# Products of row-tile pairs with seven multiplications instead of eight: which pairs take them, and where the weight sums are kept

## The chip, the core and the metric

The kernel runs on one core of a Trainium2 chip. The core has a matrix engine (TensorE, PE in the profile, with PEld for its weight loads), VectorE (DVE), ScalarE (ACT), GpSimd (POOL) and a queue engine (SyncE, SP) that issues the transfers from device memory into the on-chip buffer. Matrix products add up in a separate memory of accumulators (PSUM). The metric is the device time of one execution in microseconds. Before the change it was 2223.25 us, the median of 3 runs (2222.24 to 2224.91).

## The reference

The program is a trunk of two pre-norm layers on 256 tokens of width 2048, in float32. Each layer has a token mixer (layer 0: neighbourhood attention, layer 1: a gated short convolution) and a gated MLP with a convolution over the tokens between its two projections. A last norm closes it.

```python
def conv_glu_ffn(x, w_up, conv_w, conv_b, w_down):
    h = dwconv_centered(x @ w_up, conv_w) + conv_b      # w_up 2048 x 11264
    g, u = jnp.split(h, 2, axis=-1)
    return (jax.nn.silu(g) * u) @ w_down                # w_down 5632 x 2048

def short_conv_mixer(x, w_in, conv_w, w_out):
    gb, gc, h = jnp.split(x @ w_in, 3, axis=-1)
    return (gb * dwconv_centered(gc * h, conv_w)) @ w_out

for i in range(2):
    a = rms_norm(h, mix_norm[i])
    h = h + (neighborhood_attention(a, ...) if i == 0 else short_conv_mixer(a, ...))
    h = h + conv_glu_ffn(rms_norm(h, ffn_norm[i]), ...)
return rms_norm(h, final_norm)
```

## The kernel before

Every float32 number is held as a high and a low part, and a product of two numbers is made of three matmuls: high by high, high by low and low by high. The high part of a weight is made by ScalarE (`hi`, L122) and the low part by VectorE (`lo`, L123), out of a loaded chunk of 512 KB in one of five buffers named `raw`; `hi` and `lo` have six buffers each. `prep_to` issues the load and the splits of a chunk some steps ahead of its use (`AHEAD = 4` chunks).

Two kinds of stages follow one another. A `Phase` holds weights still and streams all tokens past them (the up-projections, L160 and L164); VectorE and ScalarE finish its columns (L213 to L225). A `Tokens` stage holds the tokens still and streams weights past them, 512 columns at a time (L336 to L338): the attention's output, the short convolution's output (`in_wscout`) and, twice in each MLP, one half of the down-projection (`in_wdown`, 22 of the 44 row tiles of the weight each). These four halves are called here L0h0, L0h1, L1h0 and L1h1, by layer and half.

A `Tokens` stage walks over two column groups (g = 0 and 1, 1024 columns each). In a group it takes its row tiles of weights two by two: 11 pairs in half an MLP, counted here from index 0, so that index 1 is the second pair. Four accumulators (`mm`: two token blocks by two halves of the columns) collect the products. A pair takes 8 products, of three matmuls each, on two chunks ("left" and "right", by columns). In a pair whose index is in a set (`S_DOWN`, L41; `S_OUT`), the 2 by 2 blocks are multiplied with seven products instead (`seven`): the two chunks are added to one another in four ways on VectorE (`sums`, L132 to L135), the tokens' sums (`forms`) were made in the stage before, and the seven products go partly into the four `mm` accumulators and partly into four more (`mu`, under the tags `st`, `sc`, `tr`, `o`). One pair after the last seven of a group, `combine` (L362 to L370) adds the four `mu` accumulators to the residual `h`. When a group's last pair is done, `residual` (L244) adds each `mm` accumulator to `h`, which frees it for the next group.

In stages that end in a norm (L0h1, `in_wscout`, the attention's output), the first group's half of the norm's input is transposed on PE into accumulators under the same four tags (L255) and scaled by VectorE and ScalarE (`scaled_split`, L200 and L201) while the second group runs. The first seven of that group needs these four accumulators back. The last half, L1h1, ends with `finale`: its last two pairs are done accumulator by accumulator, so that the final norm (`last_evac`: transposes L606, the statistic L618 to L622, its broadcast `bc` L624, eight multiplies per token block L631 and the output's transfers) can begin before the last product.

A scheduler sets each engine's order of instructions from priorities and its own estimates, so the order is not that of the code. Engines work strictly in their order.

Of the kernel before, what the change touches and what calls it, by code (L numbers as in the profile page):

```python
# [15 lines left out]
F32 = mybir.dt.float32  # L16
# [6 lines left out]
P = 128  # L23
D = 2048
S = 256
KT = D // P
# [4 lines left out]
HALF = FT // 2  # L31
# [3 lines left out]
CH = 8  # L35
# [4 lines left out]

S_DOWN = (2, 4, 6, 8)  # L41
S_OUT = (1, 3, 5)


# [10 lines left out]
def trunk(ctx, tc, xT, par, bias, wqk, wv, wo, wsc, wscout, wup, wdown, out):  # L55
    nc = tc.nc
    cp = ctx.enter_context(tc.tile_pool(name="const", bufs=1))
    wp = ctx.enter_context(tc.tile_pool(name="wts", bufs=1))
    ap_ = ctx.enter_context(tc.tile_pool(name="acts", bufs=1))
    tp = ctx.enter_context(tc.tile_pool(name="tmp", bufs=2))  # L60
# [35 lines left out]
    prepped = []  # L96
# [29 lines left out]
    def sums(l, r):  # L126

        t13 = wp.tile([P, CH * P], F32, name="raw", tag="raw", bufs=5)
        t24 = tp.tile([P, CH * P], F32, name="t24", tag="qk")
        v13, v24 = (x.rearrange("p (k f c) -> p f k c", f=4, c=P) for x in (t13, t24))  # L130
        add = nc.vector.tensor_add
        add(out=v13[:, :, 0, :], in0=l[:, :, 0, :], in1=r[:, :, 0, :])  # L132
        add(out=v13[:, :, 1, :], in0=r[:, :, 1, :], in1=r[:, :, 0, :])
        add(out=v24[:, :, 0, :], in0=v13[:, :, 0, :], in1=r[:, :, 1, :])  # L134
        add(out=v24[:, :, 1, :], in0=v24[:, :, 0, :], in1=l[:, :, 1, :])  # L135
        return parts(r[:, :, 1:2, :]), parts(t13), parts(t24)

# [132 lines left out]
    class Tokens:  # L270

        def __init__(self, parts, src, evac, sset=(), forms=None, halves=0):


            self.src, self.evac, self.sset, self.forms = src, evac, sset, forms
            self.halves = halves
            self.nk = sum(n for _, n in parts)
            for g in range(KT // 8):  # L280
                base = 0
                for w, n in parts:
                    for k0 in range(0, n, 2):
# [9 lines left out]
                        chunks.append((left, 8 * P, "cols"))  # L293
                        if k // 2 in sset:
                            chunks.append((right, 8 * P, "sums"))
                            items.append((self, g, c + 1, k, k, k + 2))
                            ends.append(c + 2)
                        else:
                            chunks.append((right, 8 * P, "cols"))
                            items.append((self, g, c, k, k, k + 2))  # L300
                            items.append((self, g, c + 1, k, k, k + 2))
                            ends.extend((c + 1, c + 2))
                    base += n

        def run(self, g, c, k0, ka, kb):
            if kb - ka > 2:
                return self.finale(g, c, ka)
            if k0 // 2 in self.sset:
                return self.seven(g, c, k0)
# [30 lines left out]
        def seven(self, g, c, k0):  # L340
            i = k0 // 2
            first, last = i == min(self.sset), i == max(self.sset)
            if first:
                self.u = [pa.tile([P, 4 * P], F32, name="mu", tag=n) for n in ("st", "sc", "tr", "o")]
            a, e, f, b = self.u
            left, (w22, t13, t24) = prepped[c - 1], prepped[c]
            fh, fl = (self.forms[i][:, j * 4 * P:(j + 1) * 4 * P] for j in range(2))
            s1, s2, s4, s3 = ((fh[:, j * P:(j + 1) * P], fl[:, j * P:(j + 1) * P]) for j in range(4))
            raw = lambda k, t: tuple(self.src[k0 + k][:, j + t * P:j + (t + 1) * P] for j in (0, S))
            for ps, x, w, j in ((a, raw(0, 0), left, 0), (self.c["11"], raw(1, 0), left, 1), (self.c["12"], s4, w22, 0),  # L350
                                (e, s1, t13, 0), (f, s3, t13, 1), (b, s2, t24, 0), (self.c["21"], raw(1, 1), t24, 1)):
                own = ps in self.u
                self.product(ps, *x, *(y[:, j * 4 * P:(j + 1) * 4 * P] for y in w[:2]), own and first, own and last)
# [298 lines left out]
    def mlp(layer, a, evac):  # L652
        for half in range(2):
# [3 lines left out]
                  intro=0 if half else 3)  # L657
            Tokens([(wdown[layer, half], HALF)], act, evac if half else residual, S_DOWN, forms,
                   halves=4 if half and layer else 0)
# [6 lines left out]
    Phase(wsc, range(3 * KT), KT, a2, sc_evac, intro=3)  # L666
    Tokens([(wscout, KT)], yT, to_norm(3, a3), S_OUT, yforms)
    mlp(1, a3, last_evac())


# [112 lines left out]
```

## Time and profile before

| what | value |
|---|---|
| median of 3 runs | 2223.25 us |
| the profiled execution, its time and its span | 2225.79 us, 2224.0 us |
| granted TensorE clock, share of full speed | 0.998 |
| PE busy | 2204.5 us, 99% |
| VectorE busy | 1748.4 us, 79% |
| ScalarE busy | 1264.9 us, 57% |
| GpSimd busy | 92.3 us, 4% |
| loads of `in_wdown` | 176 of 512 KB, median 4.8 us to landing |
| sums of weight chunks, L132 | 38, and as many of L133, L134 and L135 |

Busy time is the time in which an engine works on an instruction; the span is the time from the first instruction to the last. A row of the timeline gives the start and the duration of an instruction; in square brackets stands how long the engine had been idle before it, and what released it.

### The profile page before, as it was taken

How to read it: one execution, taken by the hardware profiler on the slowest of the kernel's cores; microseconds unless marked ns; L12 is line 12 of the kernel's file. 1: busy time of each engine (PE TensorE's matmuls, PEld its weight loads, DVE VectorE, ACT ScalarE, POOL GpSimd, SP SyncE). 2: the span in 40 equal slices, each digit the busy share in tenths (PEclk: the TensorE clock that was granted, in tenths of full speed). 3: DMA queues.
4: the chain of work that ended last, by engine and by line, in shares of the span. 5: the costliest groups of instructions: out<-in, count | busy, mean ns of one | idle time of the engine just before them, and what ended most of it. 6: DMA issues, size and time to landing. Idle time of an engine off the chain costs nothing.

```text
span 2224.0 us, 31804 instructions
## 1 busy us (share of the span) xinstructions
PE 2204.5 (99%) x11794; PEld 1902.7 (86%) x11794; DVE 1748.4 (79%) x2619; ACT 1264.9 (57%) x1881; POOL 92.3 (4%) x103
## 2 busy tenths in 40 slices
PE   9999999999999999999999999999999999999997
PEld 8888888888888888888788888888888878888886
DVE  8777665788788877888886767888787888787887
ACT  7555544656555565665564444566566555665554
POOL 1011000000100001000000000000100000001000
PEclk9999999999999999999999999999999999999999
DMA  8656555555556755665665555565566566565564
GB/s 270 191 181 184 177 172 189 181 187 192 189 169 195 232 188 180 194 190 175 182 218 191 188 189 174 180 216 189 181 194 185 175 201 218 186 192 184 170 185 137
DMA packets 214604, 421.00 MB, mean 189 GB/s; under 512 B 13488, under 2 KB 142640, under 8 KB 214448
## 3 DMA queue, kind: packets, MB, share of 16 engines
q1 hardware_dynamic: 213072, 418.33, 59.5%
q8 instruction: 93, 1.52, 0.3%
q10 hardware_dynamic: 1376, 0.63, 0.1%
q14 instruction: 63, 0.52, 0.1%
HBM read 416.81 MB, written 2.10 MB: 188 GB/s over the span
## 4 chain that ended last, share of the span: by engine, by line
PE 85%; DVE 7%; DMA 6%; issue 1%; ACT 1%; SPq 0%; DVEq 0%; ACTq 0%
PE mm L160 40%; PE mm L164 21%; DMA raw<-in_wdown 5%; PE mm L336 5%; PE mm L338 5%; PE mm L337 5%; DVE lo L123 3%; PE mm L508 1%; PE mm L510 1%; PE mm L509 1%; PE mu L336 1%; PE mu L337 1%; PE mu L338 1%; DMA raw<-in_wqk 1%; DVE t L134 0%
## 5 line engine op out<-in xcount | busy, mean ns | idle before, releaser
L122 ACT CAST hi<-raw 128x1024 fp32r<-128x1024 f32 (+1 forms) x830 | 845.2, 1022 | 576.3 <-PE mm L160 224.1
L123 DVE TENSOR_TENSOR lo<-raw,hi 128x1024 fp32r<-128x1024 f32 (+1 forms) x830 | 971.9, 1191 | 158.6 <-ACT hi L122 92.6
L160 PE MATMUL mm<-a,hi 128*128 128x512 f32 x4096 | 985.7, 391 | 1.1 <-DVE a L201 0.7
L160 PEld LDWEIGHTS mm<-a,hi 128*128 128x128 f32 x4096 | 751.2, 188 | 146.7 <-DVE a L201 1.9
L164 PEld LDWEIGHTS mm<-a,lo 128*128 128x128 f32 x4096 | 527.2, 191 | 20.9
L164 PE MATMUL mm<-a,lo 128*128 128x256 f32 x4096 | 535.2, 283 | 0.0
L225 DVE SCALAR_TENSOR_TENSOR conv<-pad,pt,conv 128x256 f32<-128x256 f32 x384 | 185.5, 484 | 157.5 <-ACT conv L223 140.7
L336 PE MATMUL mm<-hi,act 128*128 128x512 f32 x732 | 286.4, 391 | 1.5 <-DVE h L244 1.5
L338 PE MATMUL mm<-hi,act 128*128 128x512 f32 x732 | 285.7, 390 | 0.0
L337 PE MATMUL mm<-lo,act 128*128 128x512 f32 x732 | 285.1, 389 | 0.0
L336 PEld LDWEIGHTS mm<-hi,act 128*128 128x128 f32 x732 | 137.4, 188 | 30.7 <-ACT hi L122 1.7
L338 PEld LDWEIGHTS mm<-hi,act 128*128 128x128 f32 x732 | 137.4, 188 | 29.3
L337 PEld LDWEIGHTS mm<-lo,act 128*128 128x128 f32 x732 | 137.5, 188 | 29.0 <-DVE lo L123 0.4
L223 ACT ACTIVATE conv<-pad,pt 128x256 f32<-128x256 f32 x176 | 105.2, 599 | 92.6 <-DVE pad L215 92.5
L213 ACT COPY corr<-mm 128x256 f32<-128x256 f32 x256 | 94.3, 368 | 74.0 <-PE mm L164 73.5
L214 DVE TENSOR_TENSOR corr<-mm,corr 128x256 f32<-128x256 f32 x256 | 106.4, 416 | 0.0
L215 DVE TENSOR_TENSOR pad<-corr,rstd 128x256 f32<-128x256 f32 x176 | 74.1, 422 | 2.8
L384 POOL TENSOR_TENSOR s<-conv 128x128 f32<-128x128 f32 x16 | 21.0, 1312 | 1199.1 <-DVE conv L567 1199.1
L132 DVE TENSOR_TENSOR raw<-raw 128x512 f32<-128x512 f32 x38 | 26.2, 690 | 51.4 <-DMA raw<-in_wdown 49.3
L196 ACT CAST act<-conv 128x256 fp32r<-128x256 f32 x88 | 35.8, 407 | 37.8 <-DVE conv L567 37.8
L122 ACT CAST hi<-t 128x1024 fp32r<-128x1024 f32 x38 | 39.9, 1050 | 23.9 <-DVE t L135 16.6
L508 PE MATMUL mm<-hi,a 128*128 128x512 f32 x128 | 50.7, 396 | 0.0
(141 smaller groups left out, 1438.1 us busy)
## 6 DMA issues: line engine op xcount, KB each, us to landing
raw<-in_wup SPq DMA_DIRECT2D x352, 512.0 KB, 4.7
raw<-in_wdown SPq DMA_DIRECT2D x176, 512.0 KB, 4.8
raw<-in_wsc SPq DMA_DIRECT2D x96, 512.0 KB, 4.5
raw<-in_wqk SPq DMA_DIRECT2D x56, 512.0 KB, 4.3
raw<-in_wv SPq DMA_DIRECT2D x32, 512.0 KB, 4.1
raw<-in_wo SPq DMA_DIRECT2D x32, 512.0 KB, 3.5
raw<-in_wscout SPq DMA_DIRECT2D x32, 512.0 KB, 4.1
raw<-in_wqk SPq DMA_DIRECT2D x16, 256.0 KB, 5.0
```

The costliest lines, as they stand in the source:

```text
L122: nc.scalar.copy(out=hv, in_=r)
L123: nc.vector.tensor_sub(out=lv, in0=r, in1=hv.bitcast(F32))
L160: nc.tensor.matmul(ps, lhsT=prepped[i][0][:, o:o + P], rhs=self.src[k], start=k == 0, stop=False)
L164: nc.tensor.matmul(ps[:, S:], lhsT=prepped[i][1][:, o:o + P], rhs=self.src[k][:, :S], start=False, stop=k == self.nk - 1)
L213: nc.scalar.copy(out=corr, in_=ps[:, S:])
L214: nc.vector.tensor_add(out=corr, in0=ps[:, :S], in1=corr)
L215: nc.vector.tensor_mul(out=dst, in0=corr, in1=rstd)
L223: nc.scalar.activation(c, x[:, 1:S + 1], AF.Identity, scale=w[1], bias=b)
L225: nc.vector.scalar_tensor_tensor(out=c, in0=x[:, tap:tap + S], scalar=w[tap], in1=c, op0=ALU.mult, op1=ALU.add)
L336: nc.tensor.matmul(ps, lhsT=xh, rhs=wh, start=start, stop=False)
L337: nc.tensor.matmul(ps, lhsT=xh, rhs=wl, start=False, stop=False)
L338: nc.tensor.matmul(ps, lhsT=xl, rhs=wh, start=False, stop=stop)
```

## The change

The set for the down-projections moves from indices 2, 4, 6, 8 to 1, 3, 5, 7. The second group of the second half of each MLP (L0h1 and L1h1) has a set of its own, 3, 5, 7. The stage `in_wscout` keeps 1, 3, 5 in both groups. A set now belongs to a column group. The sums of weights no longer go into a fifth `raw` buffer and a temporary one, but into the two chunks themselves, after the part of the right chunk that enters a product as it is (`w22`) has been split; each of the four adds now reads what the one before it wrote.

```diff
-S_DOWN = (2, 4, 6, 8)
+S_DOWN = (1, 3, 5, 7)
 S_OUT = (1, 3, 5)
+S_LATE = (3, 5, 7)
@@
     def sums(l, r):
-        t13 = wp.tile([P, CH * P], F32, name="raw", tag="raw", bufs=5)
-        t24 = tp.tile([P, CH * P], F32, name="t24", tag="qk")
-        v13, v24 = (x.rearrange("p (k f c) -> p f k c", f=4, c=P) for x in (t13, t24))
+        w22 = parts(r[:, :, 1:2, :])
         add = nc.vector.tensor_add
-        add(out=v13[:, :, 0, :], in0=l[:, :, 0, :], in1=r[:, :, 0, :])
-        add(out=v13[:, :, 1, :], in0=r[:, :, 1, :], in1=r[:, :, 0, :])
-        add(out=v24[:, :, 0, :], in0=v13[:, :, 0, :], in1=r[:, :, 1, :])
-        add(out=v24[:, :, 1, :], in0=v24[:, :, 0, :], in1=l[:, :, 1, :])
-        return parts(r[:, :, 1:2, :]), parts(t13), parts(t24)
+        add(out=l[:, :, 0, :], in0=l[:, :, 0, :], in1=r[:, :, 0, :])
+        add(out=r[:, :, 0, :], in0=r[:, :, 1, :], in1=r[:, :, 0, :])
+        add(out=r[:, :, 1, :], in0=l[:, :, 0, :], in1=r[:, :, 1, :])
+        add(out=l[:, :, 1, :], in0=r[:, :, 1, :], in1=l[:, :, 1, :])
+        return w22, parts(l), parts(r)
@@
-                        if k // 2 in sset:
+                        if k // 2 in ssets[g]:
@@
-            left, (w22, t13, t24) = prepped[c - 1], prepped[c]
+            left, (w22, t14, t32) = prepped[c - 1], prepped[c]
@@
-                                (e, s1, t13, 0), (f, s3, t13, 1), (b, s2, t24, 0), (self.c["21"], raw(1, 1), t24, 1)):
+                                (e, s1, t14, 0), (f, s3, t32, 0), (b, s2, t32, 1), (self.c["21"], raw(1, 1), t14, 1)):
@@
-            Tokens([(wdown[layer, half], HALF)], act, evac if half else residual, S_DOWN, forms,
+            Tokens([(wdown[layer, half], HALF)], act, evac if half else residual,
+                   (S_DOWN, S_LATE if half else S_DOWN), forms,
                    halves=4 if half and layer else 0)
```

Over the whole program the pairs with seven products go from 38 to 36, and the matmuls on PE rise by 6. SP's queue issues the same loads in the same order. Most of the changed kernel's line numbers are higher by one (the adds L133 to L136, `residual` L245, `scaled_split` L202, the products L337 to L339), with `lo` at L125 and `hi` at L124.

The first place is VectorE's order at the beginning of the second column group of L0h1; the rows `a<-tr,pt,a` scale the norm's transposed input, the rows L132 to L135 are the sums for the group's first seven. Before:

```order
L123 TENSOR_TENSOR lo<-raw,hi 128x4x2x128
L132 TENSOR_TENSOR raw<-raw 128x512
L133 TENSOR_TENSOR raw<-raw 128x512
L134 TENSOR_TENSOR t_10466<-raw 128x512
L201 SCALAR_TENSOR_TENSOR a<-tr,pt,a 128x256
L135 TENSOR_TENSOR t_10466<-t_10466,raw 128x512
L201 SCALAR_TENSOR_TENSOR a<-tr,pt,a 128x256 x2
L123 TENSOR_TENSOR lo<-raw,hi 128x512
L201 SCALAR_TENSOR_TENSOR a<-tr,pt,a 128x256 x2
L123 TENSOR_TENSOR lo<-raw,hi 128x1024
L123 TENSOR_TENSOR lo<-t_10466,hi 128x1024
L201 SCALAR_TENSOR_TENSOR a<-tr,pt,a 128x256 x2
```

With the change:

```order
L245 TENSOR_TENSOR h<-mm,h 128x512 x2
L125 TENSOR_TENSOR lo<-raw,hi 128x4x2x128 x2
L202 SCALAR_TENSOR_TENSOR a<-tr,pt,a 128x256
L133 TENSOR_TENSOR raw<-raw 128x4x128
L202 SCALAR_TENSOR_TENSOR a<-tr,pt,a 128x256 x2
L134 TENSOR_TENSOR raw<-raw 128x4x128
L202 SCALAR_TENSOR_TENSOR a<-tr,pt,a 128x256 x2
L125 TENSOR_TENSOR lo<-raw,hi 128x512
L202 SCALAR_TENSOR_TENSOR a<-tr,pt,a 128x256 x2
L135 TENSOR_TENSOR raw<-raw 128x4x128
L202 SCALAR_TENSOR_TENSOR a<-tr,pt,a 128x256
L136 TENSOR_TENSOR raw<-raw 128x4x128
```

The eight rows of `a<-tr,pt,a` (L201, now L202) stood between two sets of sums and their splits, the last of them (behind this piece) after an add of the second set; now they stand among one set of sums, ahead of the splits of it.

The second place is VectorE's order where L1h0 goes from its first column group to its second; L367 to L370 are the end of `combine`, and `h<-mm,h` (L244, now L245) empties the four accumulators. Before:

```order
L367 TENSOR_TENSOR s<-mu,s 128x512
L368 TENSOR_TENSOR h<-h,s 128x512
L369 TENSOR_TENSOR h<-h,s 128x512
L370 TENSOR_TENSOR h<-h,s 128x512
L123 TENSOR_TENSOR lo<-raw,hi 128x4x2x128
L244 TENSOR_TENSOR h<-mm,h 128x512 x2
L123 TENSOR_TENSOR lo<-raw,hi 128x4x2x128
L244 TENSOR_TENSOR h<-mm,h 128x512 x2
L123 TENSOR_TENSOR lo<-raw,hi 128x4x2x128
```

With the change:

```order
L371 TENSOR_TENSOR h<-h,s 128x512
L125 TENSOR_TENSOR lo<-raw,hi 128x4x2x128 x3
L133 TENSOR_TENSOR raw<-raw 128x4x128
L134 TENSOR_TENSOR raw<-raw 128x4x128
L125 TENSOR_TENSOR lo<-raw,hi 128x512
L245 TENSOR_TENSOR h<-mm,h 128x512
L135 TENSOR_TENSOR raw<-raw 128x4x128
L245 TENSOR_TENSOR h<-mm,h 128x512
L136 TENSOR_TENSOR raw<-raw 128x4x128
L245 TENSOR_TENSOR h<-mm,h 128x512
L125 TENSOR_TENSOR lo<-raw,hi 128x4x2x128 x2
L245 TENSOR_TENSOR h<-mm,h 128x512
```

The last rows of `combine` stood right ahead of the four residual adds with one split between; now three splits and two sums of the next group stand between `combine` and the first of the four, and the four have sums and splits of the next group between them.

The third place is the end of the program. On VectorE `combine` (to L370, now L371), the residual adds (L244, now L245) and the statistic of the last norm stood thus before:

```order
L369 TENSOR_TENSOR h<-h,s 128x512
L370 TENSOR_TENSOR h<-h,s 128x512
L244 TENSOR_TENSOR h<-mm,h 128x512 x2
L638 TENSOR_REDUCE part<-ssq_105 128x1
L639 TENSOR_SCALAR part<-part 128x1
L619 TENSOR_SCALAR m<-ssq_105,part 128x1
L589 TENSOR_SCALAR a<-tr,pt 128x128
L237 RECIPROCAL m<-m 128x1
L244 TENSOR_TENSOR h<-mm,h 128x512
L589 TENSOR_SCALAR a<-tr,pt 128x128 x2
```

With the change:

```order
L371 TENSOR_TENSOR h<-h,s 128x512
L125 TENSOR_TENSOR lo<-raw,hi 128x4x2x128
L245 TENSOR_TENSOR h<-mm,h 128x512
L639 TENSOR_REDUCE part<-ssq_105 128x1
L640 TENSOR_SCALAR part<-part 128x1
L590 TENSOR_SCALAR a<-tr,pt 128x128
L245 TENSOR_TENSOR h<-mm,h 128x512
L590 TENSOR_SCALAR a<-tr,pt 128x128
```

Two residual adds stood together right behind `combine`; now a split stands behind `combine`, and the two adds are apart.

On PE the end of the products, the last norm's transposes (`tr<-pt,h`) and its first broadcast (`bc<-conv,ones`) stood thus before, down to the last matmul:

```order
L336 MATMUL mm<-hi,act 128x512
L337 MATMUL mm<-lo,act 128x512
L338 MATMUL mm<-hi,act 128x512
L336 MATMUL mm<-hi,act 128x512
L624 MATMUL bc<-conv,ones 128x128
L337 MATMUL mm<-lo,act 128x512
L338 MATMUL mm<-hi,act 128x512
L606 MATMUL tr<-pt,h 128x128 x4
L624 MATMUL bc<-conv,ones 128x128
```

With the change, from the matmul ahead of the first broadcast on:

```order
L337 MATMUL mm<-hi,act 128x512
L625 MATMUL bc<-conv,ones 128x128
L338 MATMUL mm<-lo,act 128x512
L339 MATMUL mm<-hi,act 128x512
L607 MATMUL tr<-pt,h 128x128 x4
L337 MATMUL mm<-hi,act 128x512
L338 MATMUL mm<-lo,act 128x512
L339 MATMUL mm<-hi,act 128x512
L337 MATMUL mm<-hi,act 128x512
```

The first broadcast stood ahead of the last 2 product matmuls; now 11 product matmuls and a set of four transposes are behind it.

## Rows read from the trace of the kernel before

**Rows 1.** Waits of PE: engine, line, waited for: us in total, times, longest.

```profile
PE mu L336 <- DVE a L201: 1.9, 1, 1.9
PE mm L336 <- DVE h L244: 1.5, 2, 1.3
```

**Rows 2.** Timeline of PE, L0h0: a normal pair, a seven, the next: start, duration.

```profile
652.42 0.39 PE L336 MATMUL mm<-hi,act 128*128 128x512 f32 x1
...
657.86 0.39 PE L336 MATMUL mu<-hi,act 128*128 128x512 f32 x1
...
662.72 0.40 PE L336 MATMUL mm<-hi,act 128*128 128x512 f32 x1
```

**Rows 3.** Timeline of PE at its three stalls in L0h1 and L1h0.

```profile
1064.41 0.39 PE L338 MATMUL mm<-hi,act 128*128 128x512 f32 x1
1065.05 0.47 PE L336 MATMUL mm<-hi,act 128*128 128x512 f32 x1 [0.26 <-DVE h L244]
...
1078.06 0.39 PE L337 MATMUL mm<-lo,act 128*128 128x512 f32 x1
1080.35 0.47 PE L336 MATMUL mu<-hi,act 128*128 128x512 f32 x1 [1.90 <-DVE a L201]
...
1786.71 0.39 PE L338 MATMUL mm<-hi,act 128*128 128x512 f32 x1
1788.36 0.47 PE L336 MATMUL mm<-hi,act 128*128 128x512 f32 x1 [1.26 <-DVE h L244]
```

**Rows 4.** Timeline of VectorE ahead of the second stall.

```profile
1077.98 0.69 DVE L132 TENSOR_TENSOR raw<-raw 128x512 f32<-128x512 f32 x1 [0.92 <-DMA raw<-in_wdown]
1078.59 1.22 DVE L123 TENSOR_TENSOR lo<-raw,hi 128x1024 fp32r<-128x1024 f32 x1
1079.73 0.48 DVE L201 SCALAR_TENSOR_TENSOR a<-tr,pt,a 128x256 fp32r<-128x256 f32 x1
```

**Rows 5.** Timeline of VectorE in L1h0: last seven's sums, first residual add.

```profile
1765.46 0.69 DVE L132 TENSOR_TENSOR raw<-raw 128x512 f32<-128x512 f32 x1 [3.59 <-DMA raw<-in_wdown]
...
1787.53 0.68 DVE L244 TENSOR_TENSOR h<-mm,h 128x512 f32<-128x512 f32 x1
```

**Rows 6.** Timeline of VectorE at the end of the program.

```profile
2199.63 0.68 DVE L365 TENSOR_TENSOR s<-mu,s 128x512 f32<-128x512 f32 x1
2200.34 0.69 DVE L367 TENSOR_TENSOR s<-mu,s 128x512 f32<-128x512 f32 x1
...
2202.75 0.68 DVE L244 TENSOR_TENSOR h<-mm,h 128x512 f32<-128x512 f32 x1
...
2210.29 2.06 DVE L631 TENSOR_TENSOR a<-a,bc 128x256 f32<-128x256 f32 x6
2212.28 0.68 DVE L244 TENSOR_TENSOR h<-mm,h 128x512 f32<-128x512 f32 x1
```

**Rows 7.** Timeline of PE at the end of the program.

```profile
2197.01 0.40 PE L336 MATMUL mm<-hi,act 128*128 128x512 f32 x1
...
2209.94 0.40 PE L338 MATMUL mm<-hi,act 128*128 128x512 f32 x1
2213.01 0.70 PE L606 MATMUL tr<-pt,h 128*128 128x128 f32 x4 [2.67 <-DVE h L244]
2216.32 0.80 PE L624 MATMUL bc<-conv,ones 128*128 128x128 f32 x2 [2.61 <-DVE conv L622]
```

**Rows 8.** Timeline of VectorE at the start of L0h0.

```profile
649.11 0.68 DVE L123 TENSOR_TENSOR lo<-raw,hi 128x512 fp32r<-128x512 f32 x1
649.70 0.42 DVE L215 TENSOR_TENSOR pad<-corr,rstd 128x256 f32<-128x256 f32 x1
```

**Rows 9.** Timeline of ScalarE in L1h0: the splits of a half chunk and of a sum.

```profile
1765.44 0.62 ACT L122 CAST hi<-raw 128x512 fp32r<-128x512 f32 x1 [0.44 <-DMA raw<-in_wdown]
1766.87 1.06 ACT L122 CAST hi<-raw 128x1024 fp32r<-128x1024 f32 x1 [0.81 <-DVE raw L133]
```

**Rows 10.** The loads of `in_wdown`, all 176 of them.

```profile
DMA to landing us min/median/max: 3.6/4.8/6.9
```

More of the change, by code (lines that the diff above doesn't have):

```diff
@@ L270, in trunk, with __init__ @@
     class Tokens:
-        def __init__(self, parts, src, evac, sset=(), forms=None, halves=0):
-            self.src, self.evac, self.sset, self.forms = src, evac, sset, forms
+        def __init__(self, parts, src, evac, ssets=((), ()), forms=None, halves=0):
+            self.src, self.evac, self.ssets, self.forms = src, evac, ssets, forms
             self.halves = halves
@@ L307, in run @@
                 return self.finale(g, c, ka)
-            if k0 // 2 in self.sset:
+            if k0 // 2 in self.ssets[g]:
                 return self.seven(g, c, k0)
@@ L341, in seven @@
             i = k0 // 2
-            first, last = i == min(self.sset), i == max(self.sset)
+            first, last = i == min(self.ssets[g]), i == max(self.ssets[g])
             if first:
@@ L666, in trunk @@
     Phase(wsc, range(3 * KT), KT, a2, sc_evac, intro=3)
-    Tokens([(wscout, KT)], yT, to_norm(3, a3), S_OUT, yforms)
+    Tokens([(wscout, KT)], yT, to_norm(3, a3), (S_OUT, S_OUT), yforms)
     mlp(1, a3, last_evac())
```

## The prediction

> **What bounds the kernel now.** I read the page's busy shares first: PE is busy for 2204.5 of 2224.0 us, VectorE for 79%, ScalarE for 57%, and the granted clock is 0.998 of full speed. So only two kinds of time can be won or lost: matmuls, and the 19.5 us in which PE stands still. The second view is PE's waits. Between products of the token stages they name two things: a `mu` accumulator that waits for the norm's scaling on VectorE, once, and an `mm` accumulator that waits for a residual add, twice [rows 1]. The third view is PE's timeline at these three places and at the program's end, the fourth VectorE's timeline just ahead of each, to see what the late instruction stood behind. The last views are the loads' landing times and ScalarE's splits, for the new chain that the sums make.
>
> The profiled execution took 2225.79 us, 2.54 above the median of 2223.25 us; I make the sum as a difference on that execution and subtract it from the median. A kernel that differs by under 0.2% (4.45 us: 2218.8 to 2227.7) can't be told from the one before here.
>
> **The change part by part.**
>
> Products. A normal pair takes 657.86 - 652.42 = 5.44 us and a seven 662.72 - 657.86 = 4.86 us [rows 2], so a lost seven costs 0.58 us. Two of 38 are lost, the fourth seven in the second group of L0h1 and of L1h1: **+1.16 us**. VectorE and ScalarE have less to do for them (two sets of four adds, two half splits); off the bound, I take nothing for that.
>
> The stall beside the norm's input, L0h1. PE's starts lie 2.29 us apart where the ordinary pitch is 0.23: 2.06 us are lost [rows 3]. The last of VectorE's scalings of the transposed input starts at 1079.73; ahead of it stand an add that had idled 0.92 us for a load, and a split of 1.14 us (1078.59 to 1079.73) [rows 4]. With the change the first seven comes one normal pair, 5.44 us, later, and the order has the scalings among one set of sums, not behind a second. 5.44 exceeds the 2.06 that was missing by 3.4 us, so nothing else is late there next: **-2.06 us**, from 0 (if the scalings move back by as much) to -2.06.
>
> The two column-group stalls, L0h1 and L1h0. The starts are 0.64 and 1.65 us apart, which loses 0.41 and 1.42 us [rows 3]. In L1h0 the sums of the last seven had idled 3.59 us for their load, `combine` came right ahead of the four residual adds, and the first of these began only at 1787.53, after PE had run out at 1786.71 [rows 5]. With the last seven at index 7, `combine` is due a whole pair earlier (5.44 us), so it is no longer what the residual adds stand behind. What is late next is what now stands there: the order has three splits (1.14 each) and two sums (0.6 to 0.7 each) of the next group ahead of the first residual add, about 4.7 us of VectorE, which was there to be done before as well. With PE 5.44 us to go that leaves under 1 us, so a small new wait can follow. I take **-1.83 us** for the old stalls and put new ones into a term below.
>
> The tail. In `finale`, the first two residual adds started 5.74 us after its first matmul (2202.75 - 2197.01), behind `combine` [rows 6, 7]. From them hang the statistic of the first token block and its six multiplies, which ran from 2210.29 to 2212.28; the last residual add stood behind these. It started at 2212.28, 1.94 us after the last product had ended (2209.94 + 0.40) [rows 6, 7]. Now `combine` runs a pair earlier. The first residual add can start when its 12 matmuls are done, about 2.9 us after the finale's start, the second about 6.4 us after. In the tail of before a broadcast stands 2216.32 - 2212.28 = 4.04 us behind its residual add [rows 6, 7]. So the first broadcast is ready at 6.4 + 4.04 = 10.4 us. The new order has it ahead of the last 11 product matmuls, where PE arrives after 37 matmuls at 0.23 us and two sets of transposes (0.70 each [rows 7]), at 9.8 us: PE waits some 0.65 us there. The last product then ends at 13.33 + 0.65 = 14.0 us after the finale's start, the multiplies are done by 13, and the last residual add starts at 14.0 instead of 15.27 (2212.28 - 2197.01): **-1.3 us**, what comes behind it being the same. Bounds: 0, if the add still stands behind late multiplies, and -1.9, if PE doesn't wait for the broadcast.
>
> Sums in place. Each add now reads what the one before wrote. No row shows these four in such a chain. By the nearest rows, an add starts 0.61 us after one that it doesn't need (1077.98 to the split at 1078.59 [rows 4]) and 0.71 us after one that it does (2199.63 to 2200.34 [rows 6]): 0.1 us more for each of 144 adds, 14 us of a VectorE that is idle for 21% of the span, and so nothing by itself. The Trainium skill, page "VectorE: DVE Perf Modes", section "The DRAIN you can't avoid", says that chained operations cost the same with or without a semaphore between them; by that the four would take 2.4 us and not 2.7, which differs from the rows by 0.3 us per set and moves no term here.
>
> The buffers. Before, a seven and the normal pair beside it used five of five raw buffers, now four loads share five. The right chunk of a seven goes into the buffer that the left chunk of the seven before it held, and this is free only when its sums are made and split. One round is then: landing x, the half split's 0.62 on ScalarE [rows 9] and 0.59 on VectorE (649.11 to 649.70 [rows 8]), four adds 2.8, the splits 1.06 [rows 9] and 1.14 [rows 4], and some 0.2 between engines: 6.4 us + x. PE takes 5.44 + 4.86 = 10.3 us for the two pairs. With the median landing of 4.8 us [rows 10] a round takes 11.2 and falls 0.95 us behind, three times in a group of four sevens. The reserve at the group's begin I estimate at 3 us (a pair's 5.44 us of lead less two splits of 1.14), so 2.85 us are just covered; nothing is added at the median landing.
>
> Starts of stages. With index 1 the first sums and splits of a first group come beside the last columns of the up-projection, whose last accumulator the stage needs as its fourth, 4.08 us after its first matmul. The add that frees it (L215 in [rows 8], at 649.70) has four adds and a split more before it. I place it within -0.1 to +0.6 us of the time when PE needs it, at four starts: 0 to 2.4 us. With the waits that may be new at the group changes of the MLP halves and of `in_wscout` (0 to 1 us), I take **+0.4 us**, near the lower end, as the rows of before show no wait at the 650 us start and two of 1.5 us in all at the group changes [rows 1].
>
> Sum: +1.16 - 2.06 - 1.83 - 1.3 + 0.4 = -3.6 us, 2222.2 on the profiled execution's scale, **2219.6 us** against the median.
>
> **The rivals.**
>
> A. The new early work on VectorE costs more than I take: at starts and group changes the upper ends, 3.4 us instead of 0.4. For it speaks that VectorE is 79% busy and that two of the three old stalls were such waits; against it that it works on items of the next pair that it had to do anyhow. 2219.6 + 3.0 = 2222.6 us.
>
> B. The tail doesn't shorten, since the last residual add keeps its place behind the six multiplies. For: the order still has it there. Against: the multiplies wait for the second residual add, which is freed by `combine`. 2219.6 + 1.3 = 2220.9 us.
>
> C. Slower: the round of the raw buffers. It decides from a landing of about 5.5 us in the token stages. There each round falls 1.6 to 1.7 us behind, three rounds 4.9 us, 1.9 more than the reserve; in the four first groups of the MLP halves this is 7.8 us, and 2223.25 - 3.6 + 7.8 = 2227.5 us, at the longest landing (6.9 us) throughout 6.1 per group and 24.5 us, 2244 us. For: landings reach 6.9 us [rows 10], and the loads of before were not held back by this round, so they show no queue behind it. Against: the median is 4.8, and a long landing now and then is covered in the next round. The Trainium skill, page "DMA: Bandwidth & Descriptors", section "Anatomy of one DMA — SWDGE (gpsimd) path", gives a fixed 2.0 us and bytes over 436 GB/s, for another way of issuing than this queue; 512 KB would then land in 3.2 us (an estimate by that page), a round would take 9.6 us and never fall behind. The trace differs: the shortest landing is 3.6 us [rows 10].
>
> D. The change doesn't do what it says at one place: the scalings in L0h1 are still late for the first seven. Then 2.06 us remain: 2221.7 us.
>
> E. More gain: fewer buffers in use let the loads run further ahead, and waits of PE below the ones listed vanish with them. PE stands still for 19.5 us, but most of that lies in the program's first and last microseconds, so I allow 3 us: 2216.6 us.
>
> **How the numbers follow.** Chances: the forecast 0.42, A 0.20, B 0.10, D 0.06, C 0.09, E 0.13. The forecast's own spread is about 2 us, as its two tail bounds (-1.9 and 0) and its new waits (0 to 3.4) make it, so 0.3 of it falls under 2218.8. The range takes in everything but the far ends of C and E: 2214.5 to 2225.5. Faster by over 0.2%: the low side of the forecast (0.16), most of E (0.12) and small parts of A, B and D, with a gain in one of the terms that I don't see, 0.10: 0.38. Slower: the part of C above 2227.7 and an unforeseen delay, 0.09. Within: 0.53.
>
> **What would show it.** PE's waits should no longer have the `mu` wait on the scalings and the `mm` wait on residual adds, or both under 0.3 us. The last residual add should start about 14 us after the finale's first matmul, and PE show a wait of about 0.6 us at the first `bc`. The pair pitches stay 5.44 and 4.86 us, and PE's busy time rises by about 1.2 us. C would show as waits of `mu` products on the splits, behind splits that wait for adds, behind adds that wait for loads, growing from the second seven to the fourth. A would show as waits of `mm` products on L215's accumulator or on residual adds. The prediction is wrong if PE's waits in the token stages sum to over 2 us, or if the tail's residual add keeps its 15.3 us.

## The result, and the profile after

The changed kernel took 2228.36 us, the median of 10 runs (2227.54 to 2229.87), and the kernel before 2223.86 us beside it (10 runs, 2222.24 to 2226.89): ratio 1.0017, 95% interval 1.001 to 1.0025. So it is slower by 4.5 us, where 3.6 us less was forecast, and outside the range given. In a later sitting, told below, it was 2227.57 us against 2226.23, so by 1.3 us (1.0002 to 1.0019): the sign is clear, the size depends on the kernel before, which varies between sittings.

The profiled execution of the changed kernel took 2227.54 us. The page's line of busy times:

```profile
PE 2208.6 (99%) x11800; PEld 1904.6 (86%) x11800; DVE 1750.4 (79%) x2607; ACT 1256.3 (56%) x1877; POOL 89.9 (4%) x103
```

PE has its 6 matmuls more, but is busy for 4.1 us more and not for 1.2. The waits of PE (line, waited for: us in total, times, longest):

```profile
PE mm L161 <- DVE h L245: 2.1, 1, 2.1
PE mm L337 <- DVE h L245: 1.3, 2, 1.0
PE tr L607 <- DVE h L245: 1.1, 2, 0.8
```

The `mu` wait of [rows 1] is gone, as forecast. Two of 1.3 us in all on residual adds stand at group changes again, and a wait of 2.06 us is new. They are in these places of PE's timeline (start, duration, in brackets the idle time before and its releaser): L0h0's group change, the first matmul behind the short convolution's output stage, L1h0's group change.

```profile
708.88 0.50 PE L337 MATMUL mm<-hi,act 128*128 128x512 f32 x1 [0.36 <-DVE h L245]
...
1482.79 0.47 PE L161 MATMUL mm<-a,hi 128*128 128x512 f32 x1 [2.06 <-DVE h L245]
...
1794.84 0.50 PE L337 MATMUL mm<-hi,act 128*128 128x512 f32 x1 [0.98 <-DVE h L245]
```

The stage with the new wait is the one whose pairs the change left alone. What it did change there is how the sums are made. Windows over PE in the changed kernel (stretch: its length, PE's busy time and matmuls, granted clock as a share of full speed, DMA share, GB/s) show a second price behind the wait:

```profile
1478.79:1480.79 2.00, 1.94 (x9) 1.00 0.78 246
1480.79:1482.79 2.00, 0.00 (x1) 1.00 0.25 100
1482.79:1484.79 2.00, 2.00 (x6) 0.67 0.80 252
1484.79:1486.79 2.00, 2.00 (x8) 0.50 0.58 172
1486.79:1488.79 2.00, 2.00 (x20) 0.97 0.80 193
```

After 2.06 us of standing still PE got half its clock (1.2 of 2.4 GHz) for most of 4 us. The next stage took 248.94 us instead of 247.29.

Time by stage, from the first matmul of a stage to the first of the next, in us (PE's timeline; L1h1 runs to PE's last matmul). "Output" is the short convolution's output stage, "up" the up-projection behind it. The runs of the later columns are told below; the last row is the sum of the six stages.

| stage | before | before again | changed | changed again | sets only | sums only |
|---|---|---|---|---|---|---|
| L0h0 | 115.17 | 115.18 | 116.08 | 117.00 | 115.18 | 116.31 |
| L0h1 | 119.66 | 117.60 | 117.78 | 117.78 | 117.52 | 119.23 |
| output | 85.54 | 85.53 | 88.02 | 88.52 | 85.50 | 88.01 |
| up | 247.29 | 247.29 | 248.94 | 247.42 | 247.27 | 247.40 |
| L1h0 | 117.01 | 115.69 | 116.74 | 116.25 | 115.18 | 116.19 |
| L1h1 | 126.16 | 125.74 | 125.53 | 125.12 | 124.48 | 123.63 |
| sum | 810.8 | 807.0 | 813.1 | 812.1 | 805.1 | 810.8 |

The stretch ahead of the first token stage, in which nothing is summed, took 307.3 to 310.2 us in these six traces, so the whole time of a single trace says less than its stages.

What happened in the output stage is seen on three engines. SP's queue issued these loads in the changed kernel (start, duration, engine, line):

```profile
1446.86 0.37 SPq L109 DMA_DIRECT2D raw<-in_wscout  x1
1455.93 0.37 SPq L109 DMA_DIRECT2D raw<-in_wscout  x1
1457.07 0.37 SPq L109 DMA_DIRECT2D raw<-in_wscout  x1
1458.20 0.37 SPq L109 DMA_DIRECT2D raw<-in_wscout  x1
1459.34 0.37 SPq L109 DMA_DIRECT2D raw<-in_wscout  x1
1466.28 0.37 SPq L109 DMA_DIRECT2D raw<-in_wscout  x1
1467.41 0.34 SPq L105 DMA_DIRECT2D raw<-in_wup  x1
```

The loads come in bunches with 7 to 9 us of nothing between them, and the first load of the next stage is issued 72.6 us after this stage's start (1467.41 - 1394.77). ScalarE and VectorE in the same kernel, at the sums of this stage and at its end:

```profile
1453.60 1.05 ACT L124 CAST hi<-raw 128x1024 fp32r<-128x1024 f32 x1 [2.90 <-DVE raw L136]
1463.94 1.05 ACT L124 CAST hi<-raw 128x1024 fp32r<-128x1024 f32 x1 [3.93 <-DVE raw L136]
1473.26 1.05 ACT L124 CAST hi<-raw 128x1024 fp32r<-128x1024 f32 x1 [2.24 <-DMA raw<-in_wup]
...
1474.34 1.23 DVE L125 TENSOR_TENSOR lo<-raw,hi 128x1024 fp32r<-128x1024 f32 x1 [1.47 <-ACT hi L124]
...
1480.22 0.69 DVE L371 TENSOR_TENSOR h<-h,s 128x512 f32<-128x512 f32 x1
1480.82 1.22 DVE L125 TENSOR_TENSOR lo<-raw,hi 128x1024 fp32r<-128x1024 f32 x1
1481.96 1.28 DVE L245 TENSOR_TENSOR h<-mm,h 128x512 f32<-128x512 f32 x2
```

ScalarE stood still for 2.90 and 3.93 us until the fourth add (L136) was done; its order has the split of the sums that this add completes ahead of the other one, so both wait for it, and a chunk comes free only when the sums in it are split. The next stage's first chunk came late (2.24 us of ScalarE's time), VectorE waited for its split, and behind that split stood `combine` and the residual adds that PE needed.

### The profile page after: what moved, and what is told of

It reads as the page before. It is cut to its first block, busy times and chain, and to the rows that moved or that the text cites. A ratio compares the mean times of both kernels' runs of the same rounds, so it can differ in the third digit from the quotient of the medians.

```text
span 2225.8 us, 31808 instructions
## 1 busy us (share of the span) xinstructions
PE 2208.6 (99%) x11800; PEld 1904.6 (86%) x11800; DVE 1750.4 (79%) x2607; ACT 1256.3 (56%) x1877; POOL 89.9 (4%) x103
## 4 chain that ended last, share of the span: by engine, by line
PE 91%; DVE 5%; DMA 2%; ACT 1%; issue 1%; SPq 0%; ACTq 0%; DVEq 0%
PE mm L161 41%; PE mm L165 21%; PE mm L337 6%; PE mm L339 6%; PE mm L338 6%; DVE lo L125 2%; PE mm L509 1%; PE mm L511 1%; PE mm L510 1%; PE mu L337 1%; PE mu L338 1%; PE mu L339 1%; ACT hi L124 1%; DMA raw<-in_wdown 1%; PE tr L256 1%
## 5 line engine op out<-in xcount | busy, mean ns | idle before, releaser
L124 ACT CAST hi<-raw 128x1024 fp32r<-128x1024 f32 (+1 forms) x864 | 875.5, 1024 | 616.8 <-PE mm L161 221.7
L125 DVE TENSOR_TENSOR lo<-raw,hi 128x1024 fp32r<-128x1024 f32 (+1 forms) x864 | 1008.4, 1193 | 210.4 <-ACT hi L124 139.2
L337 PE MATMUL mm<-hi,act 128*128 128x512 f32 x744 | 291.4, 392 | 1.6 <-DVE h L245 1.3
L339 PE MATMUL mm<-hi,act 128*128 128x512 f32 x744 | 290.2, 390 | 0.0
L338 PE MATMUL mm<-lo,act 128*128 128x512 f32 x744 | 289.9, 390 | 0.0
L337 PEld LDWEIGHTS mm<-hi,act 128*128 128x128 f32 x744 | 139.7, 188 | 32.7 <-DVE h L245 2.2
L339 PEld LDWEIGHTS mm<-hi,act 128*128 128x128 f32 x744 | 139.6, 188 | 29.9
L509 PE MATMUL mm<-hi,a 128*128 128x512 f32 x128 | 50.7, 396 | 0.0
L511 PE MATMUL mm<-hi,a 128*128 128x512 f32 x128 | 50.0, 390 | 0.0
L510 PE MATMUL mm<-lo,a 128*128 128x512 f32 x128 | 49.9, 390 | 0.0
```

The source lines that it names most:

```text
L124: nc.scalar.copy(out=hv, in_=r)
L125: nc.vector.tensor_sub(out=lv, in0=r, in1=hv.bitcast(F32))
L337: nc.tensor.matmul(ps, lhsT=xh, rhs=wh, start=start, stop=False)
L338: nc.tensor.matmul(ps, lhsT=xh, rhs=wl, start=False, stop=False)
L339: nc.tensor.matmul(ps, lhsT=xl, rhs=wh, start=False, stop=stop)
```

## The experiments

Theory 1 was that the sums made in place cost the time, its rival that the sets of pairs do. The kernel before itself was between 2222.8 and 2226.4 us in different sittings, so I give it with the runs of each sitting, and compare above all runs of one sitting and the stages.

**The sets alone** (all of the change but `sums`, which is that of the kernel before):

```diff
-        return w22, parts(l), parts(r)
+        return parts(r[:, :, 1:2, :]), parts(t13), parts(t24)
```

> The new sets of pairs (1,3,5,7 and 3,5,7) with the sums of the kernel before, in a fifth raw buffer and a temporary one. Theory 1, the sums made in place cost the time (both splits wait for the fourth add, the loads come later, PE waits at the end of the short convolution's output stage and the clock falls after that wait): no wait of 2 us at the end of that stage, about 2220 us, 3 to 5 us under the kernel before. Rival, the sets cost it (a seven in the second pair of a group crowds VectorE at starts and group changes): about 2228 us.

2220.38 us (before in this sitting: 2226.40); ratio 0.9972, interval 0.996 to 0.9983. The output stage has no wait. The same engines at its end:

```profile
1460.01 1.05 ACT L124 CAST hi<-raw 128x1024 fp32r<-128x1024 f32 x1 [1.82 <-DVE raw L136]
1461.82 1.05 ACT L124 CAST hi<-t 128x1024 fp32r<-128x1024 f32 x1 [0.76 <-DVE t L138]
...
1476.53 0.68 DVE L373 TENSOR_TENSOR h<-h,s 128x512 f32<-128x512 f32 x1
1477.14 1.22 DVE L125 TENSOR_TENSOR lo<-raw,hi 128x1024 fp32r<-128x1024 f32 x1
1478.27 1.28 DVE L247 TENSOR_TENSOR h<-mm,h 128x512 f32<-128x512 f32 x2
...
1462.87 0.34 SPq L105 DMA_DIRECT2D raw<-in_wup  x1
```

Here ScalarE splits the first sums after two adds (L136) while VectorE makes the other two. From the stage's start (1395.58) the next stage's first load is issued after 67.3 us, 5.3 earlier than in the changed kernel, and the first two residual adds start after 82.7 us instead of 87.2. The six stages are 5.7 us shorter than in the first trace of the kernel before and 1.9 us shorter than in its second.

**The sums alone** (the changed kernel with the old sets):

```diff
-S_DOWN = (1, 3, 5, 7)
-S_LATE = (3, 5, 7)
+S_DOWN = (2, 4, 6, 8)
+S_LATE = (2, 4, 6, 8)
```

> The old sets (2,4,6,8 in every group) with the sums made in place. Theory 1: slower than the kernel before, 2228 to 2232 us, as the old waits at the group changes of the MLP halves stay and the one at the end of the short convolution's output stage comes to them, with the clock at half for some us behind it. Rival, the sets cost it: 2222 to 2225 us and no wait at that stage's end.

2229.74 us (before: 2226.40), ratio 1.0017 (1.0008 to 1.0026), output stage 88.01 us. The wait at its end is there, but the clock stayed at 1.00 behind it (the second row is a window, with the columns of the windows above):

```profile
1486.46 0.47 PE L161 MATMUL mm<-a,hi 128*128 128x512 f32 x1 [2.03 <-DVE h L245]
...
1486.46:1488.46 2.00, 2.00 (x9) 1.00 0.68 254
```

So the main point of theory 1 holds: the sums in place bring the wait and the time, the sets don't. Two parts of its expectation missed: the clock didn't fall, and the residual adds held PE up at the ends of L0h0 and L1h0 (0.97 and 0.85 us) and not at their group changes. L1h1 is the shortest of all here, 123.63 us. It has one seven more there than with the new sets (0.58 us), and what follows PE's last matmul is 0.5 us longer. And the last residual add starts 0.04 us after the last product here too, where the kernel before had 1.94, though the sets are the old ones.

**Both kernels once more**, for a second trace.

> The kernel before once more, for a second trace of it. If the waits of its first trace are its own, the same three stalls (0.41, 2.06 and 1.42 us) stand in it; if they come and go with the loads, the time is near 2223.9 us and at least one of them is missing.

> The changed kernel once more, for a second trace of it. If the wait of 2.06 us at the end of the short convolution's output stage and the low clock behind it are its own, both stand in it, and the time is 2227.5 to 2230 us; if they come and go with the loads, the time is under 2226 us where they are missing.

The kernel before took 2225.12 us, and its waits were these:

```profile
PE mu L336 <- DVE a L201: 0.4, 1, 0.4
PE mm L336 <- DVE h L244: 0.2, 1, 0.2
```

Of the 3.89 us of stalls in [rows 3] only some 0.6 are left: those of the first trace are not in every execution. The time is all the same near that of the first trace (2225.79 us), as the stretch ahead of the first token stage took 2.4 us more. The changed kernel took 2228.29 us with 2.03 us of wait at the output stage's end, but without the fall of the clock (up stage 247.42). So the wait is its own, the fall is not.

Next I took the in-place sums apart. They do two things to the splits: both wait for the fourth add, and the chunks are held until both are done. A third effect, that an add waits for the split of the part that it overwrites, is rival 1c further down.

**The late split alone** (out of place, but grouped as in place):

```diff
-        add(out=v13[:, :, 1, :], in0=r[:, :, 1, :], in1=r[:, :, 0, :])
-        add(out=v24[:, :, 0, :], in0=v13[:, :, 0, :], in1=r[:, :, 1, :])
-        add(out=v24[:, :, 1, :], in0=v24[:, :, 0, :], in1=l[:, :, 1, :])
+        add(out=v32[:, :, 0, :], in0=r[:, :, 1, :], in1=r[:, :, 0, :])
+        add(out=v32[:, :, 1, :], in0=v14[:, :, 0, :], in1=r[:, :, 1, :])
+        add(out=v14[:, :, 1, :], in0=v32[:, :, 1, :], in1=l[:, :, 1, :])
```

> The new sets with the sums out of place, but grouped as in the changed kernel: the first tile gets the first and the fourth add, the second tile the second and third. The chunks are free after the adds as in the kernel before; only the splits wait for the third and fourth add, one more pair of adds than with the old grouping. Theory 1a, the splits that wait for the fourth add cost the time: 2226 to 2229 us, the wait of 2 to 3 us at the end of the short convolution's output stage, ScalarE waiting about 100 us for the fourth add. Rival 1b, the chunks held until their sums are split make the loads late: 2220 to 2222 us as with the sets alone, no such wait.

2220.52 us (before: 2226.10), output stage 85.95 us, far under the 2226 us that theory 1a asked for. But the run made only part of the delay that it was to make. ScalarE waited for the fourth add for 32.6 us and not for some 100 (engine, line, waited for: us in total, times, longest):

```profile
ACT hi L124 <- DVE raw L138: 32.6, 15, 3.8
```

So a late split of this size costs next to nothing by itself; one of the changed kernel's size isn't tested here.

**Earlier splits in place** (each sum split in halves behind its own add):

```diff
+        half(0, 0, l[:, :, 0, :])
         add(out=r[:, :, 1, :], in0=l[:, :, 0, :], in1=r[:, :, 1, :])
+        half(1, 0, r[:, :, 0, :])
...
+        half(1, 1, r[:, :, 1, :])
+        half(0, 1, l[:, :, 1, :])
-        return w22, parts(l), parts(r)
+        return w22, out[0], out[1]
```

> The changed kernel with each of the four sums split right behind its own add, in halves of 512 columns. The chunks are held as long as in the changed kernel. Theory 1a: the wait at the end of the short convolution's output stage goes, 2220 to 2223 us; the halves cost VectorE and ScalarE some 0.3 us more per seven, which they have. Rival 1b: 2227 to 2230 us, as the chunks still come free late.

2221.38 us, output stage 86.17 us. Rival 1b expected 2227 and more; but the halves also free the chunks earlier, since less is left to split when the fourth add is done, so this run is no proof against it (the first load of the next stage goes out 71.5 us after the stage's start, in the changed kernel 72.6 to 73.2).

**A sixth buffer** in the changed kernel:

```diff
-            raw = wp.tile([P, CH * P], F32, name="raw", tag="raw", bufs=5)
+            raw = wp.tile([P, CH * P], F32, name="raw", tag="raw", bufs=6)
```

> The changed kernel with six raw buffers instead of five (the attention's bias tile has one buffer instead of two, to make room). Theory 1a: 2226 to 2230 us, as the splits still wait for the fourth add. Rival 1b: the loads run further ahead, 2220 to 2223 us, and the wait at the end of the short convolution's output stage goes.

2222.74 us, output stage 86.49 us: 5.6 us less than the changed kernel's 2228.36. Most of the cost is bought off with one more buffer, as 1b said, though ScalarE waits for the fourth add even longer than in the changed kernel (112.0 us, below):

```profile
ACT hi L124 <- DVE raw L136: 127.9, 35, 5.0
```

So the whole late split, too, is cheap where the loads have a buffer more.

**A shorter set in the output stage** of the changed kernel:

```diff
-    Tokens([(wscout, KT)], yT, to_norm(3, a3), (S_OUT, S_OUT), yforms)
+    Tokens([(wscout, KT)], yT, to_norm(3, a3), (S_OUT, (1, 3)), yforms)
```

> The changed kernel with pairs 1 and 3 instead of 1, 3 and 5 as sevens in the second group of the short convolution's output stage. The last combine then comes two pairs earlier, and the stage's end has no sums near it. If the late combine makes the wait at this stage's end, that stage takes 85.5 + 0.58 = 86.1 us instead of 88.0 to 88.5, and the whole 2225.5 to 2226.5 us; if it is the loads of the next stage, the wait stays and the whole is 0.6 us slower than the changed kernel.

2224.93 us. The stage took 87.25 us, between the two expectations. PE doesn't wait at the stage's end any more; the seven taken away adds 0.58 us, and a wait of 0.96 us on the norm's scaling stands in the stage's middle, which the first trace of the changed kernel doesn't have and its second has with 0.60:

```profile
1447.61 0.47 PE L337 MATMUL mu<-hi,sf 128*128 128x512 f32 x1 [0.96 <-DVE a L202]
```

The run doesn't part the late combine from the late loads, as both come earlier in it: the next stage's first load goes out after 68.1 us.

**The held chunks alone**, in two runs: the first sums in a buffer of their own, so that the loads keep five; then the same with the chunks held.

```diff
-        t13 = wp.tile([P, CH * P], F32, name="raw", tag="raw", bufs=5)
+        t13 = wp.tile([P, CH * P], F32, name="t13", tag="t13", bufs=1)
...
+        for x, (_, lo) in ((l, p13), (r, p24)):
+            add(out=tp.tile([P, 1], F32, name="m", tag="m"), in0=x[:, 0, 0, :1], in1=lo[:, CH * P - 1:].bitcast(F32))
```

> The new sets with the sums out of place as in the kernel before, but the first sums' tile in a buffer of its own and not in a raw one (the attention's bias tile has one buffer instead of two, to make room). The chunks share five buffers and are free after the adds. A base for the next run: 2219 to 2221.5 us by either theory.

> The run before, with the two chunks of a seven held until their sums are split, as in the changed kernel: two additions of one column, one reading the left chunk and the last column of the first sums' low part, the other the right chunk and that of the second sums. The sums themselves and their splits wait for nothing new. Theory 1b, the chunks held until their sums are split make the loads late and bunch them: 2224 to 2229 us, with PE waits at the end of the short convolution's output stage or at group changes of 3 us or more in all. Rival 1c, it is the chain of the adds made in place (the third add waits for the split of the part it overwrites, and both splits for the fourth add) that makes ScalarE and VectorE late: within 1.5 us of the run before.

2221.05 us and 2223.01 us (before in this sitting: 2222.84; ratios 0.9992, 0.9984 to 1.0001, and 1.0005, 0.9996 to 1.0014). Held chunks cost 2.0 us, less than theory 1b asked for and more than its rival 1c; by stage 0.8 in L1h0 and 0.0 in the output stage. Neither part alone, as far as these runs made it, brings the wait of 2 us.

**Both parts together**, out of place (the late split's `sums` with `t14` in a buffer of its own, and the two holding additions behind it), beside the changed kernel.

> The two single parts put together, out of place: the sums grouped with the first and the fourth add in one tile (a buffer of its own), and the two chunks held until their sums are split. What this leaves out of the changed kernel is only the third and the first add's wait for the splits of the parts that they overwrite. Theory 2, late splits and held chunks cost the time only together: 2226 to 2229 us, 2 to 3 us of wait at the end of the short convolution's output stage. Rival 1c, the wait of the adds for the splits of what they overwrite is the rest: 2222.5 to 2224.5 us, as with the held chunks alone, and under 1 us of wait at that stage's end.

> The changed kernel on the same chip and beside the same runs of the kernel before, as the measure for the run above, since the kernel before has been between 2222.8 and 2226.4 us in different sittings: 2227.5 to 2229.5 us by every theory.

2232.84 us (6 runs, 2232.07 to 2234.30) against 2227.57 for the changed kernel and 2226.23 for the kernel before. The output stage took 89.66 us and L0h0 117.24, where the parts alone had 85.95 and 85.51, and 115.18 and 115.32. In this kernel the queue of these loads waited for the holding additions, and ScalarE for the fourth add (engine, line, waited for: us in total, times, longest):

```profile
SPq L109 <- DVE m L141: 304.8, 60, 11.6
...
ACT hi L124 <- DVE t L138: 90.1, 27, 5.5
```

So late splits and held chunks cost the time together, and rival 1c, which wanted 2222.5 to 2224.5 us here, falls as the main cause. Theory 2 missed too, as the time is 4 us above its range. The wait at the output stage's end was 3.29 us here, on a split of ScalarE, and the up stage behind it took 248.97 us. Why both together stand 5 us above the changed kernel is open. One thing is seen in a seven of the output stage: the first holding addition stands behind both splits of the sums, and the second behind one split more, so the chunks are held some 1.1 us longer than those two splits ask for (1462.27 to 1463.41):

```profile
1459.92 2.36 DVE L125 TENSOR_TENSOR lo<-t,hi 128x1024 fp32r<-128x1024 f32 x2 [1.20 <-ACT hi L124]
1462.20 0.15 DVE L141 TENSOR_TENSOR m<-raw,lo 128x1 f32<-128x1 f32 x1
1462.27 1.22 DVE L125 TENSOR_TENSOR lo<-raw,hi 128x1024 fp32r<-128x1024 f32 x1
1463.41 0.15 DVE L141 TENSOR_TENSOR m<-raw,lo 128x1 f32<-128x1 f32 x1
```

The loads tell the same story. From the output stage's start, the next stage's first load goes out after 67.3 us with the sets alone, 69.3 with the late split, 70.0 with the held chunks, 72.6 to 73.2 in the changed kernel and 74.3 with both parts; PE waits at the stage's end in the last two.

**The late set taken away**, with the sums of the kernel before:

```diff
-S_LATE = (3, 5, 7)
+S_LATE = (1, 3, 5, 7)
```

> The new sets with the sums of the kernel before, and the late set of the second half's second group taken away: 1, 3, 5, 7 there too, beside the norm's input. If the first seven in the group's second pair needs the four accumulators before the norm's scaling has left them, PE waits there in L0h1, and the stage takes 119 us or more instead of 117.5, against 0.58 us won by the seven that is added: 2221.5 to 2224 us. Rival, the scheduler moves other products ahead and the scaling is in time, as in the short convolution's output stage, which has the same set: 116.9 us for the stage, and about 2219.5 us.

2222.02 us (before: 2225.73). L0h1 took 117.77 us instead of 117.52, so 0.83 us of new waiting ate the 0.58 of the added seven; L1h1 took 125.03 instead of 124.48. PE waits there for the norm's scaling, as the first expectation had it, but for 0.59 us in L0h1, so the stage lies between the two expectations. The late set is worth 0.8 us in the stages.

## Why the prediction was wrong

- The step that failed is the term of the sums in place and of the buffers: "a VectorE that is idle for 21% of the span, and so nothing by itself" and "nothing is added at the median landing". Its price beside the new sets is 7 to 8 us, changed kernel less sets alone (2228.36 - 2220.38, or 2227.57 - 2220.38 by the last sitting); by the six stages it is 6.9 to 8.8 us in the three traces.
- Beside the old sets the same sums cost 3.3 us (2229.74 - 2226.40), so the two halves don't add up: -6.0 and +3.3 make -2.7, and the whole is 1.3 to 4.5 us slower. The tail's gain of 1.9 us (below) is in both halves and counts once; the rest isn't explained.
- The adds' own time was judged rightly, though not for the reason given ahead of the prediction, that each add reads what the one before it wrote. By the diff only the fourth does; the second and the third overwrite what the add before them read. They wait for it all the same: 0.72 us from start to start (1786.21 and 1786.93 in L1h0), where 0.71 was taken.
- I had counted this time and not what waits for the adds. Before, the first sums' tile was whole after two adds and ScalarE split it beside the other two; in place, no tile is whole before the third add, and the first one not before the fourth. Over the program ScalarE waited for it 33 times:

```profile
ACT hi L124 <- DVE raw L136: 112.0, 33, 5.7
```

- The round of the buffers was set up rightly (landing and 6.4 us against PE's 10.3) and its falling behind too, but the reserve of 3 us was an estimate with no row behind it, and I looked for the price in the wrong place: in `mu` products of the MLP halves, from landings of 5.5 us on. It came at landings of 4.8 us (`in_wdown`, median of before and after), as VectorE that is late at the end of a group, with `combine` and residual adds in line behind late splits. L1h0 shows it at its plainest: ScalarE's split waits 5.74 us for the fourth add, VectorE's splits wait for that one, and the last residual add, which PE needs, starts behind them:

```profile
1790.73 1.05 ACT L124 CAST hi<-raw 128x1024 fp32r<-128x1024 f32 x1 [5.74 <-DVE raw L136]
...
1791.82 2.36 DVE L125 TENSOR_TENSOR lo<-raw,hi 128x1024 fp32r<-128x1024 f32 x2 [0.60 <-ACT hi L124]
1794.10 0.68 DVE L245 TENSOR_TENSOR h<-mm,h 128x512 f32<-128x512 f32 x1
```

- The order shown ahead of the prediction had this: in its piece at L1h0 two splits stand ahead of the last residual add. I had counted what stands ahead of the first one.
- The output stage, 2.5 to 3.0 us longer in the three traces of the changed kernel and in the one with the sums alone, stood in the forecast with "0 to 1 us", and with its group change only. Its pairs were the same, so I read the change as not touching it.
- The sign of being wrong came: PE's waits in the token stages and at the end of one sum to 3.4 us, over the 2 us named. They are on residual adds, which was rival A's sign, at A's group changes and at a place that A didn't have. Rival C came nearest by time (2227.5 us) and named the held buffers, but its sign, `mu` products that wait for splits, isn't there.
- The sets gain, as forecast, but by how much isn't settled: 6.0 us by the medians of one sitting, 1.8 in another (with the first sums in a buffer of their own, 2221.05 against 2222.84), where my terms without the sums came to 3.6. The stall beside the norm's input went (L0h1 119.66 or 117.60, now 117.52), those at the group changes too in the sets-only run (L1h0 117.01 or 115.69, now 115.18). But the size rested on one trace: by the second one these stalls were worth 0.6 us and not 3.89. That the forecast lies between 1.8 and 6.0 is in part luck.
- The tail shortened by 1.9 us, the end of the bounds and not the 1.3 taken. It does so with the sums alone and the old sets too, so an earlier `combine` isn't the only way to it. In the changed kernel the last residual add starts 0.04 us after the last product's end (2213.67 + 0.39), before 1.94 us [rows 6, 7]. PE didn't wait for the broadcast, which was ready 3.4 us behind the second residual add and not 4.04:

```profile
2207.17 0.69 DVE L245 TENSOR_TENSOR h<-mm,h 128x512 f32<-128x512 f32 x1 [1.10 <-PE mm L339]
2214.10 0.69 DVE L245 TENSOR_TENSOR h<-mm,h 128x512 f32<-128x512 f32 x1 [0.22 <-PE mm L339]
...
2210.60 0.38 PE L625 MATMUL bc<-conv,ones 128*128 128x128 f32 x1
2213.67 0.39 PE L339 MATMUL mm<-hi,act 128*128 128x512 f32 x1
```

- Three slips of arithmetic moved nothing: a round falls 6.4 + 4.8 - 10.3 = 0.9 us behind and not 0.95, PE comes to the broadcast after 37 x 0.23 + 2 x 0.70 = 9.9 us and not 9.8, and 0.3 of 0.42 is 0.13 and not 0.16.

The fastest version is the sets alone, 2220.38 us, with the late split out of place (2220.52 us) as good as level.

## What to carry to other kernels

When a result moves into the place of its operands, ask what was free between the two before: here ScalarE split half the sums while VectorE made the other half, and the loads refilled the operands meanwhile. In the runs a part of the first cost 0.1 us (2220.52 against 2220.38), the second 2.0, and both together in the changed kernel 7 to 8; so price a change of buffers by when each buffer is free and by who can start then, not by the instructions. And read a stall of a few tenths of a per cent from two traces before you book its removal.

## What was not expected of the hardware

PE stood still for 2 us or more at the end of the output stage in five traces. In the first of the changed kernel (2.06 us) the granted clock then fell to 0.50 (windows above) and the next stage took 1.65 us longer. In its third (2.33 us) the clock fell to 0.50 and the next stage took 248.97 us as well, and so it was with both parts together (3.29 us). With the sums alone (2.03 us) the clock stayed at 1.00, and so it did in the second trace of the changed kernel (2.03 us), as the windows there show (same columns as above):

```profile
1481.95:1483.95 2.00, 1.97 (x9) 1.00 0.74 268
1483.95:1485.95 2.00, 0.00 (x1) 1.00 0.13 53
1485.95:1487.95 2.00, 2.00 (x9) 1.00 0.75 254
1487.95:1489.95 2.00, 2.00 (x20) 1.00 0.63 182
```

So in some executions such a wait costs nearly twice its length; what decides it, these traces don't show. The stall of 1.90 us at the norm's input before [rows 3] left it at 1.00 too.
